# Adaptive-norm columns in fewer, wider tiles, with the projection pieces spread over the next tile and TensorE's order fixed

## The chip, the cores and the metric

One Trainium2 chip, one core. The metric is the device time of one execution in microseconds (us). The kernel before took 1053.7 us (median of 3 runs, 1052.96 to 1055.31).

## The reference

One decoder layer on 256 tokens of width 2048: an adaptive norm, a fused input projection, four attention mixers, an output projection, and a mixture of 16 experts. What the change touches is the beginning:

```python
c_act = jax.nn.silu(c)
mod = c_act @ ada_w[l] + ada_b[l]                    # (1, 2048) @ (2048, 12288)
sh1, sc1, g1, sh2, sc2, g2 = jnp.split(mod, 6, axis=-1)
h = rmsnorm(x, norm1_g[l]) * (1.0 + sc1[:, None]) + sh1[:, None]
proj = h @ w_in_l                                    # the first step of token_mixer
```

All is float32. sc1 and sh1 are matrix-vector products with 2048 x 2048 weights each; h must be complete in a 128-wide block of the width before that block can enter the projection.

## The kernel before

**The early stage.** The width of 2048 is 16 blocks k of 128. The loop over j = 0 to 7 makes two blocks of sc1 and two of sh1 at a time: `ada_tile` (L288) cuts the 2048 x 256 weights of such a tile into 4 units of 512 KB, each with 4 contraction blocks of 256 columns (rows of 1 KB in memory). `ada_acc` (L484) multiplies a unit: for each contraction block k one fp32 matmul with c as the 32-wide stationary operand, placed at column position 32 * (k % 4) of the array, so that the four blocks of a unit stand on four positions. All 16 blocks of a tile add up in one PSUM bank, "ada", which has one buffer. ScalarE copies the sum out (L501), `ada_cols` (L515) adds the four partial sums in small matmuls, and VectorE turns them into columns (L522), adds the bias (L523) and, for sc1, the gain (L526). In the loop `ada_cols` also takes its bank from "ada" (ATAG).

**The hidden state.** `norm1` makes the token norms, `x_transposes` turns x into blocks xT, and `hidden` applies scale and shift and splits each block into a high part Hh and a low part Hl.

**Early pieces.** While the columns are made, TensorE already multiplies finished blocks with parts of the input projection: `early_unit` k is 1024 columns of w_in for one block (rows of 4 KB), and the tiles 4 and SIXTH of w_in come in pieces of 4 blocks by 256 columns (rows of 1 KB). Each piece is split into high and low (`halves`: ScalarE L584, VectorE L586) into two buffers, and `three` (L558) issues three full-width matmuls for each product: 24 matmuls a piece, 23 pieces in all. `bias_tiles` i (16 of them, 16 matmuls each, bank "S") build the attention bias and have no part in the columns. Of the two buffers of "S" one is held by an early accumulator.

**Loads.** All weights come in one list of units, in the order of use, on the SyncE queue into a ring of 11 slots of 512 KB. A slot is free when its unit has been multiplied (columns) or split (pieces); the next load of the list then goes out.

**Order.** The program is written in the order of the loops. A scheduler places the instructions of each engine at build time with a simulated timeline; instructions that are ready in it go first, earlier ones of the program ahead of later ones. `behind` adds an edge of order between two instructions without a wait. `Batch` uses it to keep the matmuls of a unit together. Nothing ties one unit to the next, or to the pieces. The stage ends with the loop's last pieces (blocks 14 and 15, and the last piece of tile 4); then come the gate columns of mixer D (L704) and the rest of the projection.

Of the kernel before, what the change touches and what calls it, by code (L numbers as in the profile page):

```python
# [21 lines left out]
S = 256  # L22
# [158 lines left out]
def hybrid_trunk_kernel(  # L181
# [8 lines left out]
    def behind(ins, other):  # L190

        tc.add_manual_dep(ins, other.name, mybir.DependencyInfo(
            mybir.DependencyClass.NoSync, mybir.DependencyReason.DATA), reason="order")

    class Batch:

        prev = None

        def __call__(self, op, *args, **kw):
            if self.prev is None:  # L200
                ins = op(*args, **kw).ins  # L201
            else:
                with tc.high_priority():
                    ins = op(*args, **kw).ins  # L204
                behind(ins, self.prev)
            self.prev = ins

# [79 lines left out]

    def ada_tile(key):  # L288
        return ada_units(acol[key[0]] + 256 * key[1], key, 256, 4)

# [8 lines left out]
    units = []  # L299
    for j in range(8):  # L300
        units += ada_tile(("sc1", j))
        if j == 0:
            units += [(None, lambda t=t: nc.sync.dma_start(x0[t], x[0, 128 * t:128 * t + 128, :])) for t in range(2)]
        units += [early_unit(2 * j)] + ada_tile(("sh1", j)) + [early_unit(2 * j + 1)]
        if j % 2:
            units.append(win_units(4)[j // 2])
        elif j:
            units.append(win_units(SIXTH)[j // 2 - 1])

# [248 lines left out]
    def three(o, wh, wl, hh, hl, first, last, wstat):  # L558

        if wstat:  # L560
            ins = mm(o, wl, hh, start=first, stop=False)  # L561
            mm(o, wh, hl, start=False, stop=False)  # L562
            mm(o, wh, hh, start=False, stop=last)  # L563
        else:
            ins = mm(o, hh, wl, start=first, stop=False)  # L565
            mm(o, hl, wh, start=False, stop=False)  # L566
            mm(o, hh, wh, start=False, stop=last)  # L567
        return ins.ins
# [53 lines left out]

    def hidden(j):
        for k in (2 * j, 2 * j + 1):
            hs = attp.tile([128, 256], F32, name="hs", tag="hs", bufs=2)
            V.tensor_scalar(hs, xT[:, k, :], A1[:, k:k + 1], B1[:, k:k + 1], OP.mult, OP.add)
            A.copy(Hh[:, k, :], hs[:])
            V.tensor_tensor(Hl[:, k, :], hs[:], Hh[:, k, :].bitcast(F32), OP.subtract)

    for j in range(8):  # L630
        ev = None
        for u in range(4):
            ev = ada_acc(("sc1", j), [u], ev, 4, 256)
        if j == 0:
            norm1()
        else:
            early_mms(2 * j - 2)
        x_transposes(2 * j)
        bias_tiles(2 * j)
        ada_cols(ev, 2, A1[:, 2 * j:2 * j + 2], 16 + 2 * j, g1n[:, 2 * j:2 * j + 2], tag=ATAG)  # L640
        early_split(2 * j)
        ev = None
        for u in range(4):
            ev = ada_acc(("sh1", j), [u], ev, 4, 256)
        bias_tiles(2 * j + 1)
        ada_cols(ev, 2, B1[:, 2 * j:2 * j + 2], 2 * j, tag=ATAG)
        hidden(j)
        if j:
            early_mms(2 * j - 1)
        if j and j % 2 == 0:  # L650
            early_mms5(4, j // 2 - 1)
        early_split(2 * j + 1)
        if j % 2:
            if j > 1:
                early_mms5(SIXTH, j // 2 - 1)
            early_split5(4, j // 2)
        elif j:
            early_split5(SIXTH, j // 2 - 1)
    for k in (14, 15):
        early_mms(k)  # L660
    early_mms5(4, 3)

# [1010 lines left out]
```

## Time and profile before

| | |
|---|---|
| median of 3 runs | 1053.7 us |
| profiled execution | 1056.39 us, span 1054.6 us |
| TensorE busy | 960.3 us, 91% of the span |
| weight loads of TensorE | 582.9 us |
| VectorE busy | 500.4 us, 47% |
| ScalarE busy | 353.1 us, 33% |
| moved by DMA | 371.14 MB, mean 352 GB/s |

The span goes from the first to the last instruction of one profiled execution; the time of that execution is 1.8 us longer. PE is TensorE's matmuls, DVE VectorE, ACT ScalarE, SP SyncE (SPq its DMA queue). Matmuls are pipelined and their ends modelled, so one row's duration is longer than the distance to the next row. TensorE records an fp32 matmul with a 32-wide or 64-wide stationary operand as two passes, that is two rows.

### The profile page before, as it was taken

Reading aid. Unit: us, or ns where it says so; the run is one execution under the profiler, and the core shown is the slowest. Engines: PE = TensorE matmul, PEld = TensorE weight load, DVE = VectorE, ACT = ScalarE, POOL = GpSimd, SP = SyncE. Lnnn points to the kernel's source line nnn. Section 1 sums busy time; section 2 is a strip of 40 time slices with the busy share of each in tenths; the row PEclk is TensorE's granted clock in tenths of the full one; section 3 lists DMA queues with packets and bytes.
Section 4 is the critical chain, followed back from the end, with each engine's and each line's share of the span. In section 5 each row is a group of like instructions: output and inputs, shape, how many; then the busy total and the mean of one; then the engine's idle time right before and its main releaser. Section 6 shows DMA issues by size and latency. Waiting matters only on the chain.

```text
span 1054.6 us, 16417 instructions
## 1 busy us (share of the span) xinstructions
PE 960.3 (91%) x6465; PEld 582.9 (55%) x6465; DVE 500.4 (47%) x1006; ACT 353.1 (33%) x763; POOL 4.8 (0%) x14
## 2 busy tenths in 40 slices
PE   5899999999999998989998999999889897899994
PEld 1677778898788985656784433433243232433323
DVE  2444566996998998344445231414024040422215
ACT  3333344566776768534444101100010000200013
POOL 0000000000000000000000000000000000000000
PEclk9999999999999999999998999999999999999998
DMA  9999999996999999889653999999999999999994
GB/s 332 357 358 359 357 323 325 355 373 210 335 325 348 325 384 387 307 270 384 228 214 145 341 421 414 412 417 415 422 407 421 412 420 413 419 419 414 421 359 128
DMA packets 153596, 371.14 MB, mean 352 GB/s; under 512 B 11514, under 2 KB 90275, under 8 KB 136875
## 3 DMA queue, kind: packets, MB, share of 16 engines
q1 hardware_dynamic: 152512, 368.41, 94.2%
q10 hardware_dynamic: 938, 1.61, 0.4%
q8 instruction: 53, 0.87, 0.3%
q14 instruction: 29, 0.23, 0.1%
q0 software_dynamic: 64, 0.02, 0.0%
HBM read 367.91 MB, written 2.10 MB: 351 GB/s over the span
## 4 chain that ended last, share of the span: by engine, by line
PE 66%; DMA 15%; DVE 8%; ACT 5%; issue 4%; SPq 0%; DVEq 0%; ACTq 0%
PE dn L201 10%; DMA ugu<-in_exp_w_up_dram 9%; PE acc L561 5%; PE acc L562 4%; PE acc L563 4%; PE gatep L201 4%; PE upp L201 3%; PE ada L201 3%; PE upp L204 3%; DMA r<-in_exp_w_up_dram 3%; PE oacc L565 3%; PE pg L1410 3%; PE oacc L566 3%; PE oacc L567 3%; PE gatep L204 2%
## 5 line engine op out<-in xcount | busy, mean ns | idle before, releaser
L561 PE MATMUL acc<-Hh,wlo 128*128 128x256 f32 x512 | 145.7, 294 | 6.3 <-DVE wlo L586 3.9
L562 PE MATMUL acc<-Hl,whi 128*128 128x256 f32 x512 | 146.1, 288 | 0.0
L563 PE MATMUL acc<-Hh,whi 128*128 128x256 f32 x512 | 145.2, 286 | 0.0
L586 DVE TENSOR_TENSOR wlo<-r,whi 128x1024 fp32r<-128x1024 f32 x85 | 103.8, 1221 | 62.7 <-ACT whi L584 60.1
L584 ACT CAST whi<-r 128x1024 fp32r<-128x1024 f32 x85 | 88.9, 1047 | 77.2 <-PE acc L563 28.7
L561 PEld LDWEIGHTS acc<-Hh,wlo 128*128 128x128 f32 x512 | 96.3, 192 | 16.9 <-DVE wlo L586 7.0
L562 PEld LDWEIGHTS acc<-Hl,whi 128*128 128x128 f32 x512 | 98.6, 193 | 3.5 <-issue 2.6
L563 PEld LDWEIGHTS acc<-Hh,whi 128*128 128x128 f32 x512 | 98.6, 193 | 2.7 <-issue 2.3
L511 DVE SCALAR_TENSOR_TENSOR ada_v<-r,cT,ada_v 128x1024 f32<-128x1024 f32 x75 | 95.9, 1279 | 0.4
L204 PE MATMUL upp<-ugu,xg 128*64 128x512 f32 x220 | 90.7, 597 | 4.4 <-DMA ugu<-in_exp_w_up_dram 4.4
L1464 DVE TENSOR_TENSOR he<-upp,sg 128x128 f32<-128x128 f32 x32 | 7.1, 282 | 180.0 <-PE upp L204 180.0
L204 PE MATMUL gatep<-ugu,xg 128*64 128x512 f32 x192 | 82.2, 601 | 0.5 <-DMA ugu<-in_exp_w_gate_dram 0.5
L1543 ACT CAST yhl<-yo 128x512 fp32r<-128x512 f32 x31 | 19.1, 618 | 164.1 <-DVE yo L1537 136.8
L204 PE MATMUL gatep<-r,xg 128*64 128x512 f32 x176 | 71.1, 596 | 0.9 <-DMA r<-in_exp_w_gate_dram 0.9
L201 PE MATMUL dn<-udh,heT 128*64 128x512 f32 x140 | 68.0, 599 | 1.0 <-DVE heT L1481 1.0
L1494 DVE TENSOR_TENSOR xt<-xt,sco 128x512 f32<-128x512 f32 (+1 forms) x70 | 42.1, 637 | 55.4 <-PE sco L1493 54.9
L204 PE MATMUL upp<-r,xg 128*64 128x512 f32 x148 | 65.7, 596 | 2.6 <-DMA r<-in_exp_w_up_dram 2.6
L204 PE MATMUL dn<-udh,heT 128*64 128x512 f32 x140 | 67.6, 599 | 0.0
L1460 ACT ACTIVATE sg<-gatep 128x512 f32<-128x512 f32 x8 | 4.8, 597 | 167.9 <-PE gatep L204 167.9
L565 PE MATMUL oacc<-wlo,Oh 128*128 128x512 f32 (+1 forms) x160 | 58.8, 369 | 0.2
L201 PE MATMUL dn<-r,heT 128*64 128x512 f32 (+1 forms) x124 | 55.5, 558 | 1.6 <-DVE heT L1481 1.6
L567 PE MATMUL oacc<-whi,Oh 128*128 128x512 f32 (+1 forms) x160 | 56.8, 355 | 0.0
(404 smaller groups left out, 1909.0 us busy)
## 6 DMA issues: line engine op xcount, KB each, us to landing
r<-in_ada_w_dram SPq DMA_DIRECT2D x156, 512.0 KB, 7.6
udh<-in_exp_w_down_dram SPq DMA_DIRECT2D x70, 512.0 KB, 11.4
r<-in_w_in_dram SPq DMA_DIRECT2D x69, 512.0 KB, 7.3
ugu<-in_exp_w_up_dram SPq DMA_DIRECT2D x34, 1024.0 KB, 14.6
ugu<-in_exp_w_gate_dram SPq DMA_DIRECT2D x33, 1024.0 KB, 13.8
r<-in_exp_w_gate_dram SPq DMA_DIRECT2D x31, 1024.0 KB, 13.0
r<-in_exp_w_up_dram SPq DMA_DIRECT2D x30, 1024.0 KB, 14.3
r<-in_exp_w_down_dram SPq DMA_DIRECT2D x56, 512.0 KB, 11.4
```

Source lines behind the costliest of these rows:

```text
L201: ins = op(*args, **kw).ins
L204: ins = op(*args, **kw).ins
L511: V.scalar_tensor_tensor(acc, w, cT[:, u:u + 1], acc[:], OP.mult, OP.add)
L561: ins = mm(o, wl, hh, start=first, stop=False)
L562: mm(o, wh, hl, start=False, stop=False)
L563: mm(o, wh, hh, start=False, stop=last)
L565: ins = mm(o, hh, wl, start=first, stop=False)
L566: mm(o, hl, wh, start=False, stop=False)
L567: mm(o, hh, wh, start=False, stop=last)
L584: A.copy(hi, w)
L586: V.tensor_tensor(lo, w, hi[:].bitcast(F32), OP.subtract)
L1494: V.tensor_tensor(y(t, cs), y(t, cs), o, OP.add)
```

## The change

The first norm columns come in five tiles, two of 256 columns and three of 512 (TILES). A unit stays at 512 KB: of a wide tile it has 2 contraction blocks of 512 columns, rows of 2 KB, and there are 8 units each for sc1 and sh1. The pieces of a tile's blocks are no longer issued beside the next units of the same loop, but spread among the units of the next tile by `tile_plan`: a piece is loaded and split ahead of a unit and multiplied behind it. The pieces of the last tile (five) follow at the end. `ada_cols` takes its bank from "S". `chained` ties TensorE's units and pieces into one order, that of the loads: the first matmul of each goes behind the last of the one ahead. Transposes follow units n and n + 2 of a tile (n units each for sc1 and sh1), bias tiles the odd units, up to 4, 6, 9, 12 and 16 by the end of each tile.

```diff
--- before.py
+++ after.py
@@ -192,6 +192,15 @@
         tc.add_manual_dep(ins, other.name, mybir.DependencyInfo(
             mybir.DependencyClass.NoSync, mybir.DependencyReason.DATA), reason="order")
 
+    chain = [None, False]
+
+    def chained(ins, first=False):
+
+        if chain[1]:
+            if first and chain[0] is not None:
+                behind(ins, chain[0])
+            chain[0] = ins
+
     class Batch:
 
         prev = None
@@ -199,10 +208,12 @@
         def __call__(self, op, *args, **kw):
             if self.prev is None:
                 ins = op(*args, **kw).ins
+                chained(ins, True)
             else:
                 with tc.high_priority():
                     ins = op(*args, **kw).ins
                 behind(ins, self.prev)
+                chained(ins)
             self.prev = ins
 
 
@@ -285,8 +296,38 @@
 
     acol = {"sh1": 0, "sc1": 2048, "g1": 4096, "sh2": 6144, "sc2": 8192, "g2": 10240}
 
-    def ada_tile(key):
-        return ada_units(acol[key[0]] + 256 * key[1], key, 256, 4)
+
+    TILES = ((0, 2), (2, 2), (4, 4), (8, 4), (12, 4))
+
+    def ada_tile(nm, t):
+        k0, n = TILES[t]
+        return ada_units(acol[nm] + 128 * k0, (nm, t), 128 * n, 8 // n)
+
+    def tile_pieces(t):
+
+        if t < 0:
+            return []
+        k0, n = TILES[t]
+        ps_ = [("e", k) for k in range(k0, k0 + n)]
+        if (k0 + n) % 4 == 0:
+            ps_.insert(1, ("w", 4, k0 // 4))
+            if k0 < 12:
+                ps_.insert(3, ("w", SIXTH, k0 // 4))
+        return ps_
+
+    def piece_unit(p):
+        return early_unit(p[1]) if p[0] == "e" else win_units(p[1])[p[2]]
+
+    def tile_plan(t):
+
+        n = 2 * TILES[t][1]
+        adas = [(nm, u) for nm in ("sc1", "sh1") for u in range(n)]
+        pcs = tile_pieces(t - 1)
+        plan = []
+        for i, a in enumerate(adas):
+            plan += [p for q, p in enumerate(pcs) if (q + 1) * 2 * n // (len(pcs) + 1) == i]
+            plan.append(("a", i) + a)
+        return plan
 
     def ada_block(key):
         nm, b, width = key
@@ -297,15 +338,12 @@
                                               [(nm, 2 * h, 512), (nm, 2 * h + 1, 512)])]
 
     units = []
-    for j in range(8):
-        units += ada_tile(("sc1", j))
-        if j == 0:
-            units += [(None, lambda t=t: nc.sync.dma_start(x0[t], x[0, 128 * t:128 * t + 128, :])) for t in range(2)]
-        units += [early_unit(2 * j)] + ada_tile(("sh1", j)) + [early_unit(2 * j + 1)]
-        if j % 2:
-            units.append(win_units(4)[j // 2])
-        elif j:
-            units.append(win_units(SIXTH)[j // 2 - 1])
+    for t in range(len(TILES)):
+        for it in tile_plan(t):
+            units.append(ada_tile(it[2], t)[it[3]] if it[0] == "a" else piece_unit(it))
+            if t == 0 and it[2:] == ("sc1", 3):
+                units += [(None, lambda t=t: nc.sync.dma_start(x0[t], x[0, 128 * t:128 * t + 128, :])) for t in range(2)]
+    units += [piece_unit(p) for p in tile_pieces(len(TILES) - 1)]
 
     nw = len(wtiles)
     wkeys = [u[0] for i in range(NEARLY, nw) for u in win_units(i)[3 * (i == SIXTH):]]
@@ -560,11 +598,13 @@
         if wstat:
             ins = mm(o, wl, hh, start=first, stop=False)
             mm(o, wh, hl, start=False, stop=False)
-            mm(o, wh, hh, start=False, stop=last)
+            end = mm(o, wh, hh, start=False, stop=last)
         else:
             ins = mm(o, hh, wl, start=first, stop=False)
             mm(o, hl, wh, start=False, stop=False)
-            mm(o, hh, wh, start=False, stop=last)
+            end = mm(o, hh, wh, start=False, stop=last)
+        chained(ins.ins, True)
+        chained(end.ins)
         return ins.ins
 
     zero = attp.tile([128, 512], BF, name="zero")
@@ -620,45 +660,63 @@
                 P.transpose(pt[:, i, 128 * t:128 * t + 128], x0[t][:, 128 * (k + i):128 * (k + i) + 128], ident)
         V.tensor_tensor(xT[:, k:k + 2, :], pt[:], rxb[:].unsqueeze(1).broadcast_to([128, 2, 256]), OP.mult)
 
-    def hidden(j):
-        for k in (2 * j, 2 * j + 1):
+    def hidden(k):
+        if True:
             hs = attp.tile([128, 256], F32, name="hs", tag="hs", bufs=2)
             V.tensor_scalar(hs, xT[:, k, :], A1[:, k:k + 1], B1[:, k:k + 1], OP.mult, OP.add)
             A.copy(Hh[:, k, :], hs[:])
             V.tensor_tensor(Hl[:, k, :], hs[:], Hh[:, k, :].bitcast(F32), OP.subtract)
 
-    for j in range(8):
-        ev = None
-        for u in range(4):
-            ev = ada_acc(("sc1", j), [u], ev, 4, 256)
-        if j == 0:
-            norm1()
-        else:
-            early_mms(2 * j - 2)
-        x_transposes(2 * j)
-        bias_tiles(2 * j)
-        ada_cols(ev, 2, A1[:, 2 * j:2 * j + 2], 16 + 2 * j, g1n[:, 2 * j:2 * j + 2], tag=ATAG)
-        early_split(2 * j)
-        ev = None
-        for u in range(4):
-            ev = ada_acc(("sh1", j), [u], ev, 4, 256)
-        bias_tiles(2 * j + 1)
-        ada_cols(ev, 2, B1[:, 2 * j:2 * j + 2], 2 * j, tag=ATAG)
-        hidden(j)
-        if j:
-            early_mms(2 * j - 1)
-        if j and j % 2 == 0:
-            early_mms5(4, j // 2 - 1)
-        early_split(2 * j + 1)
-        if j % 2:
-            if j > 1:
-                early_mms5(SIXTH, j // 2 - 1)
-            early_split5(4, j // 2)
-        elif j:
-            early_split5(SIXTH, j // 2 - 1)
-    for k in (14, 15):
-        early_mms(k)
-    early_mms5(4, 3)
+    def split_piece(p):
+        early_split(p[1]) if p[0] == "e" else early_split5(p[1], p[2])
+
+    def piece_products(p):
+        early_mms(p[1]) if p[0] == "e" else early_mms5(p[1], p[2])
+
+    def scale_cols(t, ev):
+        k0, n = TILES[t]
+        ada_cols(ev, n, A1[:, k0:k0 + n], 16 + k0, g1n[:, k0:k0 + n], tag="S")
+
+    def shift_cols(t, ev):
+        k0, n = TILES[t]
+        ada_cols(ev, n, B1[:, k0:k0 + n], k0, tag="S")
+        for k in range(k0, k0 + n):
+            hidden(k)
+
+    chain[1] = True
+    bias_at, made = (4, 6, 9, 12, 16), 0
+    for t, (k0, nblk) in enumerate(TILES):
+        ev, pend, n = None, None, 2 * nblk
+        for it in tile_plan(t):
+            if it[0] != "a":
+                split_piece(it)
+                pend = it
+                continue
+            i, nm, u = it[1:]
+            if u == 0:
+                ev = None
+            ev = ada_acc((nm, t), [u], ev, 8 // nblk, 128 * nblk)
+            if pend:
+                piece_products(pend)
+                pend = None
+            if t == 0 and i == n - 1:
+                norm1()
+            if i == n - 1:
+                scale_cols(t, ev)
+            if i == 2 * n - 1:
+                shift_cols(t, ev)
+            if i in (n, n + 2) and i - n < nblk:
+                x_transposes(k0 + i - n)
+            if i % 2 and made < bias_at[t]:
+                bias_tiles(made)
+                made += 1
+    rest = tile_pieces(len(TILES) - 1)
+    split_piece(rest[0])
+    for q, p in enumerate(rest):
+        if q + 1 < len(rest):
+            split_piece(rest[q + 1])
+        piece_products(p)
+    chain[1] = False
 
 
     qkv = {}
```

## Rows read from the trace of the kernel before

**Rows 1.** The page, busy tenths of 40 slices of the span:
```profile
PE   5899999999999998989998999999889897899994
...
DMA  9999999996999999889653999999999999999994
```

**Rows 2.** Stretches: length, busy PE, PEld, DVE, ACT, POOL, clock, DMA share, GB/s:
```profile
0.00:50.00 50.00, 33.50 (x329) 18.51 (x330) 18.40 (x57) 19.23 (x41) 1.73 (x8) 0.97 1.02 344
30.00:130.00 100.00, 93.51 (x1116) 70.62 (x1108) 44.53 (x102) 34.80 (x69) 0.00 (x0) 0.98 1.09 358
385.00:410.00 25.00, 24.64 (x194) 19.40 (x194) 24.71 (x45) 19.06 (x47) 0.00 (x0) 1.00 1.05 386
40.00:60.00 20.00, 17.76 (x216) 12.91 (x206) 8.41 (x19) 6.67 (x14) 0.00 (x0) 0.91 1.09 357
```

**Rows 3.** Who TensorE waited for, 20 to 160 us: total, times, longest:
```profile
PE ada L201 <- DMA r<-in_ada_w_dram: 6.6, 3, 5.9
PE ada L201 <- DVE ada_ev L522: 2.5, 4, 0.9
...
PE ada_c L520 <- ACT ada_ev L501: 2.0, 3, 0.9
...
PE S L553 <- DVE xT L621: 1.3, 1, 1.3
PE xtr L620 <- DVE TD L556: 1.2, 2, 0.7
```

**Rows 4.** Timeline of TensorE: start, duration, line, operation, idle before:
```profile
20.38 0.61 PE L201 MATMUL ada<-r,cB 128*32 128x256 f32 x1 [5.85 <-DMA r<-in_ada_w_dram]
...
44.20 0.61 PE L201 MATMUL ada<-usc,cB 128*32 128x256 f32 x1 [1.29 <-DVE B L523]
```

**Rows 5.** Who the SyncE queue waited for, 20 to 160 us:
```profile
SPq L219 <- PE ada L204: 31.8, 28, 4.5
```

**Rows 6.** Timeline of TensorE, end of the early stage:
```profile
145.06 0.39 PE L204 MATMUL ada<-r,cB 128*32 128x256 f32 x3
145.99 0.32 PE L520 MATMUL ada_c<-ada_ev,kc 128*32 128x64 f32 x8 [0.54 <-ACT ada_ev L501]
148.38 0.74 PE L561 MATMUL acc<-Hh,wlo 128*128 128x256 f32 x4 [2.07 <-ACT Hh L627]
...
157.21 1.92 PE L704 MATMUL gacc<-Hh,uw 128*24 128x256 f32 x30
```

**Rows 7.** Who TensorE waited for, 157 to 240 us:
```profile
PE acc L561 <- DVE wlo L586: 1.4, 1, 1.4
```

**Rows 8.** Timeline of TensorE, a column unit between products:
```profile
60.05 0.28 PE L563 MATMUL acc<-Hh,whi 128*128 128x256 f32 x1
...
60.26 0.42 PE L204 MATMUL ada<-r,cB 128*32 128x256 f32 x3
...
60.50 0.39 PE L204 MATMUL ada<-r,cB 128*32 128x256 f32 x3
...
60.83 0.38 PE L561 MATMUL acc<-Hh,wlo 128*128 128x256 f32 x1
```

**Rows 9.** Timeline of TensorE, a bias tile between two column units:
```profile
83.03 0.54 PE L553 MATMUL S<-tabs,line 105*128 105x32 bf16 x15
83.50 0.40 PE L201 MATMUL ada<-r,cB 128*32 128x256 f32 x1
```

**Rows 10.** Timeline of TensorE, two passes of two 512-column matmuls, experts:
```profile
568.06 0.59 PE L201 MATMUL gatep<-ugu,xg 128*64 128x512 f32 x1
...
568.49 0.59 PE L201 MATMUL gatep<-ugu,xg 128*64 128x512 f32 x1
```

**Rows 11.** Timeline of TensorE, two neighbouring 512-column units of g1:
```profile
405.79 0.62 PE L201 MATMUL ada<-ug,cB 128*32 128x512 f32 x1
...
405.81 0.62 PE L204 MATMUL ada<-r,cB 128*32 128x512 f32 x2
406.25 0.59 PE L201 MATMUL ada<-ug,cB 128*32 128x512 f32 x1
```

## The prediction

> **What bounds the kernel now.** I read the page's slices first, then stretches of the early stage, then who waits for whom there, then the instructions themselves. In the slices [rows 1], of 26.4 us each, the DMA engines are at 9 tenths in the first nine and TensorE from the third on, and the change lies in the first six. So one must ask which of the two ends last.
>
> The loads run at 358 GB/s from 30 to 130 us with the DMA share over 1 [rows 2]: saturated. TensorE is busy 93.5 of those 100 us [rows 2], and its waits between 20 and 160 us are short and mostly on VectorE and ScalarE; the waits for a load come to 6.6 us [rows 3], 5.9 of them one wait that ends at 20.4 us [rows 4]. The SyncE queue, in turn, waits 31.8 us in 28 pieces for TensorE to give back a column slot [rows 5]. So after about 26 us no landing holds TensorE up, while TensorE's pace holds issues up: TensorE is the bound by a little, with the loads close behind. The end shows it too: the last column unit ends near 145.3 us, the three remaining pieces run from 148.4 to 157.2 us, and the next stage follows without a gap [rows 6]; from 157 to 240 us TensorE waits 1.4 us in all [rows 7]. A microsecond more or less at 157 us is therefore carried on, through a TensorE stage into the experts, whose loads start as buffers come free.
>
> **Prices.** A column unit of 256 columns is four fp32 matmuls, one on each 32-column position of the array. The four start together, and a second pass of all four follows 0.24 us later [rows 8]; in a run of such units each takes 0.43 us. Where a unit stands between products of full width, the way in costs 0.09 us and out 0.12 us (60.05 + 0.12 to 60.26, and 60.50 + 0.21 to 60.83) [rows 8]: 0.21 us a run. Products of a piece are 24 at 0.12 us, 2.9 us a piece: three pieces fill 148.38 to 157.2 us [rows 6]. A bias tile between two units takes 0.47 us for 15 of its 16 matmuls (83.03 to 83.50) [rows 9], 0.57 us with the turn.
>
> **The change, part by part.**
>
> *Wider units.* A 512-column unit of the same bytes holds two contraction blocks, so only two of the four positions. Two 512-column matmuls side by side take 0.43 us a pass, two passes each (the experts' rows at 568.06 and 568.49) [rows 10]: 0.86 us a unit, double. Only if the next unit, with the other two positions, follows directly do the four run together: two such units of different loads at 405.79 us start within 0.02 us and take two passes of about 0.45 us for both [rows 11]. So 48 units cost 48 x 0.43 = 20.6 us now and 20.6 to 41.3 us after.
>
> How many can pair? The new plan puts products behind units 3, 6, 9, 12 of the third tile and behind 2, 4, 6, 9, 11, 13 of the last two, and between units 7 and 8 the accumulator is copied out. Taking neighbours greedily, the third tile needs 10 turns of 0.86 us (6 pairs, 4 alone), each of the last two 9 (7 pairs, 2 alone): 28 turns, 24.1 us. But the loop also places bias tiles behind units 1, 3, 5 (and 7), and transposes behind 8 and 10, and these split pairs: in strict program order 11 + 13 + 13 = 37 turns, 31.8 us. In the trace some such fillers stand between two column units [rows 9] and others elsewhere, so I take the middle, 33 turns: 28.4 us, **+7.7 us** (bounds +3.5 and +11.2).
>
> *Loads.* 48 of the 87 units go from rows of 1 KB to rows of 2 KB. The stretch 385 to 410 us, in which 512-column blocks with rows of 2 KB dominate, ran at 386 GB/s against 358 GB/s [rows 2]. Subtracting the 4 KB rows of the sixteen wide pieces, I estimate 350 GB/s for 1 KB rows: 48 x 0.524 MB at 350 and at 386 GB/s is 71.9 and 65.2 us, 6.7 us sooner. TensorE is the bound, so this goes into loads that lie ready in the eleven slots, and I cost it at **nothing**; the cover is TensorE's backlog, and if that were gone the 6.7 us would count.
>
> The Trainium skill ("DMA: Bandwidth & Descriptors", "Specifications") gives 512 B as the minimum transfer for line rate. By it 1 KB rows would have lost nothing, and the load term would be zero in every case; the two rates in [rows 2] disagree.
>
> *Spread pieces and their order.* The same 23 pieces of 2.9 us are multiplied; five instead of three are left behind the last column unit (14.5 against 8.8 us). As TensorE is the bound, that is work moved, not added. On the SyncE queue the same 87 loads are issued, five instead of two behind the last column unit. At the start: up to the second tile's last column unit the new queue has 18 units and x, some 12 MB with the constants; at 344 GB/s (0 to 50 us) [rows 2] they land by 35 to 38 us. TensorE then has 16 column units and two pieces behind it, as at 41 us now: **0**. Six bias tiles instead of three are done by then, in time that waits for loads anyway: 3 x 0.57 = **-1.7 us**.
>
> *Column turns.* Ten turns instead of sixteen, each with a copy out and a small matmul group. The waits at turns now are 2.5 + 2.0 us [rows 3] and the last turn's, the rest covered by pieces. After, no piece may fill in, as the chain fixes the order; behind a waiting column unit all of TensorE's chained work queues. The last turn waited 0.54 us for a 256-column copy [rows 6]; with 512 columns I estimate 0.8 us, so six wide and two narrow turns wait 5.9 us against some 5: **0**, within 2 us either way.
>
> *Other waits.* The 1.2 us for the bias bank [rows 3] should fall away with one bank of its own for the columns: **-1.2 us**, at most -2.5 with the 1.3 us on xT. The granted clock was 0.91 from 40 to 60 us [rows 2]; TensorE had waited 1.29 us before 44.20 us [rows 4], and at the lower of its two levels, 1.2 for 2.4 GHz, 0.09 x 20 = 1.8 us are lost. The same thin stretch exists after, so I take half: **-0.9 us**. The longer chain at the end (copy and group of 512 columns): **+0.3 us**.
>
> Sum: 7.7 - 1.7 - 1.2 - 0.9 + 0.3 = **+4.2 us** at the end of the early stage, passed on. The profiled execution took 1056.39 us (span 1054.6, 1.8 around it): 1060.6 us against it. It stood 2.7 us over the median, so the prediction is 1053.7 + 4.2 = 1057.9 us.
>
> **Rivals.**
>
> *Faster: the pairs hold and the order pays.* At 28 turns, with the fillers placed in the copy-out waits (-2), all of -2.5 and -1.8: 3.5 - 1.7 - 2.5 - 1.8 - 2.0 + 0.3 = -4.2 us, 1049.5 us. If TensorE then keeps up with the loads, up to the 6.7 us can show: 1047 us. For it: 6.5 us of idle between 30 and 130 us [rows 2] that a better order could use. Against it: fillers in program order. It decides below about 29 turns.
>
> *No change.* The early stage moves by a few us, and the stage behind it gives that back: loads lie further ahead, so VectorE can take its weight and column work in the longer tail. Against it: TensorE is at 9 tenths or more there [rows 1] with 1.4 us of waits [rows 7]. 1053.7 us, within 2.
>
> *Neighbours don't overlap.* If the second unit's first pass can only follow the first unit's first pass, two adjacent units take three passes, 1.29 us, not two. The 15 pairs among 48 units in 33 turns then cost 15 x 0.43 = 6.5 us more: +10.7, 1064.4 us. The start times in [rows 11] speak against it. The Trainium skill ("TensorE: Matmul & The Clock Gate", Part 3, "The mechanism") says that matmuls start and end strictly in program order, without reordering; emitted unit by unit this is what that would do, and the trace agrees only if the four were laid out pass by pass.
>
> *The clock stays low.* TensorE would wait for loads between 23 and 41 us, and after a wait the unit at 44.20 us took 0.61 us a pass where others take 0.40 [rows 4, 8]; two pieces at the lower level are 5.8 us more of work, of which I let some 3.6 reach the end: 1061.5 us. I count it into the upper part of the range.
>
> **How the numbers follow.** Part of the pairs (the forecast) 0.37, with its own range 1055 to 1061.5; neighbours that don't overlap, or no pairs at all, 0.13; no change 0.20; faster 0.30. A difference under 0.2% (2.1 us) cannot be told from none. The forecast and the non-overlap case are slower: 0.50; same 0.20; faster 0.30. The range runs from 1048.5 (the favourable case with some of the loads' gain) to 1064.5 us (non-overlap).
>
> **What would show it.** In the profile after: 512-column units with passes 0.43 us apart, alone (0.86 us) or four matmuls together; some 33 turns; loads near 370 GB/s and the slot wait of the SyncE queue larger, not smaller; no long load waits of TensorE after 41 us; last column unit near 142 us, first matmul of the next stage near 161 us instead of 157.2. Wrong, if TensorE waits for landings throughout (then the loads were the bound), if the next stage starts before 156 us, or if that shift is not found again at the first expert matmul.

## The result, and the profile after

The changed kernel took 1084.65 us (median of 4 runs, 1082.34 to 1088.05) against 1054.51 us for the kernel before: a ratio of 1.0272 (95% interval 1.0240 to 1.0304), 30 us slower. The forecast was 1057.9 us in a range of 1048.5 to 1064.5 us: the direction was right, the size far too small. The profiled execution has a span of 1081.0 us, 26.4 us more than before: 11.3 us are lost by the first matmul of the gate columns, 10.9 from there to the output projection, 2.5 to the experts and 1.7 behind them.

The page of the changed kernel, TensorE and DMA in the slices [rows 1]:

```profile
PE   5798989699899999897998999899879898898994
...
DMA  9998998689799999988853899999999999999993
```

(Slices of 27.0 us.) Stretches as in [rows 2], with the same columns, and one of the stage that follows:

```profile
0.00:50.00 50.00, 32.57 (x320) 17.81 (x324) 16.28 (x52) 18.82 (x41) 1.74 (x8) 0.93 1.01 343
30.00:130.00 100.00, 89.14 (x826) 62.48 (x825) 41.96 (x87) 30.76 (x57) 0.00 (x0) 0.93 0.98 341
40.00:60.00 20.00, 17.73 (x208) 13.04 (x209) 7.72 (x19) 7.05 (x14) 0.00 (x0) 0.90 1.01 361
190.00:230.00 40.00, 30.74 (x270) 27.18 (x269) 26.59 (x56) 18.05 (x33) 0.53 (x1) 0.87 0.69 236
```

Who TensorE waited for, 26.3 to 168 us [rows 3], and below it the SyncE queue, 20 to 160 us [rows 5]:

```profile
PE acc L599 <- ACT Hh L667: 3.8, 4, 1.9
PE acc L600 <- DVE Hl L668: 2.3, 3, 1.0
PE ada_c L558 <- ACT TD L594: 1.7, 1, 1.7
PE ada_c L558 <- DVE xT L661: 1.7, 2, 0.9
PE S L591 <- DVE ada_ev L560: 1.6, 4, 0.5
PE ada L210 <- ACT ada_ev L539: 1.5, 3, 0.7
PE ada_c L558 <- ACT ada_ev L539: 1.5, 2, 0.7
PE S L591 <- DVE xT L661: 0.5, 1, 0.5
```

```profile
SPq L230 <- PE ada L214: 44.6, 21, 7.1
SPq L295 <- PE ada L214: 18.1, 7, 3.6
```

No row names a landing, as none did in the kernel before after 26.3 us. The 14.6 us (10.4 in the kernel before, from 26.3 us to its gate columns) are what surrounds a column turn: the copies, the columns, then the hidden halves Hh and Hl, then the first products. The waits for TD and xT (3.9 us) are for bank "S": the bias tiles and the transposes of x, which the columns now share it with, had to be copied out of it first. And the SyncE queue waits longer for TensorE's column units (44.6 + 18.1 us in the two rows shown, against 31.8 us in [rows 5] and 3.7 us in a row not shown there), so the loads run slower from 30 to 130 us, 341 against 358 GB/s. The timeline of TensorE, at the first turns and at the end of the stage [rows 6]:

```profile
13.05 0.61 PE L591 MATMUL S<-tabs,line 105*128 105x32 bf16 x16
...
24.09 1.19 PE L518 MATMUL S<-dg,ones 128*128 128x128 f32 x4 [1.37 <-DVE dg L517]
...
26.07 0.44 PE L558 MATMUL ada_c<-ada_ev,kc 128*32 128x64 f32 x8
...
33.72 0.44 PE L558 MATMUL ada_c<-ada_ev,kc 128*32 128x64 f32 x8 [1.68 <-ACT TD L594]
...
35.80 0.58 PE L599 MATMUL acc<-Hh,wlo 128*128 128x256 f32 x1 [0.69 <-ACT Hh L667]
37.16 0.58 PE L600 MATMUL acc<-Hl,whi 128*128 128x256 f32 x1 [0.78 <-DVE Hl L668]
37.54 0.41 PE L601 MATMUL acc<-Hh,whi 128*128 128x256 f32 x1
37.76 0.41 PE L599 MATMUL acc<-Hh,wlo 128*128 128x256 f32 x1
...
147.64 0.59 PE L210 MATMUL ada<-r,cB 128*32 128x512 f32 x1
147.64 0.59 PE L214 MATMUL ada<-r,cB 128*32 128x512 f32 x1
147.65 0.59 PE L210 MATMUL ada<-r,cB 128*32 128x512 f32 x1
147.66 0.59 PE L214 MATMUL ada<-r,cB 128*32 128x512 f32 x1
...
152.06 0.38 PE L599 MATMUL acc<-Hh,wlo 128*128 128x256 f32 x1 [1.92 <-ACT Hh L667]
...
168.46 0.85 PE L762 MATMUL gacc<-Hh,uw 128*24 128x256 f32 x12
```

The first scale columns wait behind a bias tile and the token norms, which have bank "S" ahead of them: they come at 26.07 us. In the kernel before the same matmuls stood in bank "ada" at 14.08 us:

```profile
14.08 0.44 PE L520 MATMUL ada_c<-ada_ev,kc 128*32 128x64 f32 x8 [0.49 <-ACT ada_ev L501]
```

The shift columns at 33.72 us wait 1.68 us for that bank again. From there to 37.16 us one turn costs TensorE the three waits shown and 0.37 us ahead of a bias tile, and the products after them come 0.21 us apart instead of 0.12 us until 40.3 us: the lower of the two clock levels (granted 0.50). Stretches of the changed kernel at that level:

```profile
33.80:40.50 6.70, 4.86 (x40) 4.32 (x41) 3.44 (x9) 2.32 (x5) 0.00 (x0) 0.50 1.08 373
54.30:57.60 3.30, 3.18 (x14) 3.01 (x15) 1.15 (x4) 1.06 (x4) 0.00 (x0) 0.50 1.03 402
85.00:88.30 3.30, 3.30 (x17) 3.28 (x16) 2.11 (x4) 1.49 (x3) 0.00 (x0) 0.50 1.08 374
153.20:156.50 3.30, 3.30 (x18) 3.30 (x17) 2.95 (x5) 0.68 (x2) 0.00 (x0) 0.50 1.12 340
```

Each begins in or behind the waits of a shift turn. Together they are 17 us; the kernel before has one such stretch, of 3.4 us (44.2 to 47.6 us). The four rows at 147.64 us are two neighbouring 512-column units that overlap on all four positions, as [rows 11] had it. The stage ends at 168.46 us, 11.3 us later than before.

Then as much again is lost. TensorE and, below it, the SyncE queue from 200 us on:

```profile
213.87 1.09 PE L941 MATMUL pcTp<-ident,pc 128*128 128x128 f32 x4 [6.65 <-DVE vc L901]
216.23 0.58 PE L599 MATMUL acc<-Hh,wlo 128*128 128x256 f32 x1 [1.27 <-DVE wlo L626]
```

```profile
200.86 0.38 SPq L248 DMA_DIRECT2D uw<-in_w_in_dram  x1
211.54 0.38 SPq L248 DMA_DIRECT2D r<-in_w_in_dram  x1
```

That is mixer D's compression, whose small steps TensorE, VectorE and ScalarE pass to each other. From the vcp matmuls (206.8 us) to these transposes TensorE has no piece; in the kernel before three stood there (191.0 to 202.7 us). No load goes out for 10.7 us, TensorE stands for 6.65 us, and the stretch from 190 to 230 us moves 236 GB/s. From the gate columns to the output projection TensorE's waits of over 0.15 us come to 18.2 us, against 8.1 us before: 10.1 of the 10.9 us.

### The profile page after: what moved, and what is told of

It reads as the page before. It is cut to its first block, busy times and chain, and to the rows that moved or that the text cites. A ratio compares the mean times of both kernels' runs of the same rounds, so it can differ in the third digit from the quotient of the medians.

```text
span 1081.0 us, 15910 instructions
## 1 busy us (share of the span) xinstructions
PE 968.8 (90%) x6225; PEld 584.3 (54%) x6225; DVE 501.5 (46%) x991; ACT 355.6 (33%) x759; POOL 4.8 (0%) x14
## 4 chain that ended last, share of the span: by engine, by line
PE 68%; DMA 15%; DVE 8%; ACT 5%; issue 3%; SPq 0%; ACTq 0%; DVEq 0%
PE dn L210 10%; DMA ugu<-in_exp_w_up_dram 7%; PE acc L599 5%; PE acc L600 4%; PE acc L601 4%; PE gatep L210 4%; PE ada L210 4%; PE upp L210 4%; PE upp L214 3%; DMA r<-in_exp_w_up_dram 3%; PE oacc L603 3%; PE pg L1468 3%; PE oacc L604 3%; PE oacc L605 3%; PE gatep L214 3%
## 5 line engine op out<-in xcount | busy, mean ns | idle before, releaser
L599 PE MATMUL acc<-Hh,wlo 128*128 128x256 f32 x512 | 154.9, 303 | 8.3 <-DVE wlo L626 4.4
L600 PE MATMUL acc<-Hl,whi 128*128 128x256 f32 x512 | 149.3, 292 | 2.4 <-DVE Hl L668 2.3
L601 PE MATMUL acc<-Hh,whi 128*128 128x256 f32 x512 | 148.8, 291 | 0.0
L626 DVE TENSOR_TENSOR wlo<-r,whi 128x1024 fp32r<-128x1024 f32 x81 | 98.9, 1222 | 59.1 <-ACT whi L624 59.0
L599 PEld LDWEIGHTS acc<-Hh,wlo 128*128 128x128 f32 x512 | 101.5, 198 | 26.6 <-issue 10.7
L624 ACT CAST whi<-r 128x1024 fp32r<-128x1024 f32 x81 | 84.5, 1048 | 85.3 <-PE acc L601 24.3
L600 PEld LDWEIGHTS acc<-Hl,whi 128*128 128x128 f32 x512 | 101.6, 198 | 3.6 <-DVE Hl L668 3.5
L601 PEld LDWEIGHTS acc<-Hh,whi 128*128 128x128 f32 x512 | 101.4, 198 | 1.6 <-issue 1.6
L210 PE MATMUL dn<-udh,heT 128*64 128x512 f32 x140 | 69.5, 612 | 0.5 <-DVE heT L1539 0.5
L214 PE MATMUL dn<-udh,heT 128*64 128x512 f32 x140 | 69.1, 612 | 0.0
L210 PE MATMUL ada<-r,cB 128*32 128x512 f32 (+1 forms) x140 | 53.2, 587 | 9.9 <-DMA r<-in_ada_w_dram 8.2
L214 PE MATMUL ada<-r,cB 128*32 128x512 f32 (+1 forms) x244 | 59.8, 583 | 0.0
## 6 DMA issues: line engine op xcount, KB each, us to landing
ugu<-in_exp_w_up_dram SPq DMA_DIRECT2D x34, 1024.0 KB, 14.7
ugu<-in_exp_w_gate_dram SPq DMA_DIRECT2D x33, 1024.0 KB, 13.7
```

What stands on the lines that cost most here:

```text
L601: end = mm(o, wh, hh, start=False, stop=last)
L624: A.copy(hi, w)
L626: V.tensor_tensor(lo, w, hi[:].bitcast(F32), OP.subtract)
```

## The experiments

Three landmarks are the starts of TensorE's first matmul of the gate columns (end of the early stage), of the output projection and of the experts. The medians stand beside those of the kernel before on the same chip.

```
                      us      before   ratio (95%)             gate   output  experts
before                1054.5                                   157.2  401.8   561.2
after                 1084.7  1054.5   1.0272 (1.0240-1.0304)  168.5  424.0   585.9
e1_no_chain           1074.6  1056.2   1.0157 (1.0117-1.0197)  168.2  417.9   577.6
e2_chain_before       1051.8  1056.2   0.9948 (0.9922-0.9974)  151.0  399.2   556.7
e3_narrow_tiles       1086.9  1056.2   1.0278 (1.0238-1.0318)  180.0  432.0   590.4
e4_transposes_later   1079.7  1056.2   1.0190 (1.0147-1.0233)  169.0  427.0   585.6
e5_products_at_turns  1060.9  1056.9   1.0031 (1.0012-1.0050)  159.5  407.3   565.2
e6_at_turns_narrow    1077.8  1056.9   1.0168 (1.0130-1.0207)  174.7  425.1   585.1
e7_extra_matmuls      1087.5  1056.9   1.0268 (1.0232-1.0304)  182.4  437.9   596.8
e8_one_piece_later    1069.3  1056.5   1.0122 (1.0082-1.0163)  165.8  413.2   572.9
e9_stream_first       1085.3  1056.5   1.0269 (1.0230-1.0308)  168.7  423.8   586.2
e10_turns_other_bank  1063.1  1056.5   1.0059 (1.0028-1.0091)  160.5  407.4   566.0
e11_steps_on_time     1075.5  1054.3   1.0208 (1.0176-1.0239)  169.2  414.7   579.6
e12_half_loads_after  1087.6  1054.3   1.0309 (1.0279-1.0339)  179.2  433.3   592.5
e13_half_loads_before 1052.6  1054.3   0.9966 (0.9944-0.9988)  141.1  397.4   557.5
```

TensorE's time from 26.3 us to the gate columns by what it works on, from the first run of rows that starts behind 26.3 us, each run counted up to the start of the next (a few matmul records are missing). A wait ahead of a run is therefore part of the run before it. The last two columns are TensorE's waits of over 0.15 us, those ahead of piece products and all:

```
            units  columns  bias tiles  transposes  pieces  (ahead of pieces, all waits)
before      32.2   12.0      8.7        4.4         73.2    2.1  10.4
after       36.9    6.6     11.5        6.2         80.4    6.2  14.6
e1          45.3    7.0     10.5        5.6         73.3    5.8  12.7
e2          33.8    8.3      8.2        5.4         68.8    0.0   7.5
e3          43.7    7.1     12.8        6.0         83.8    6.9  24.9
e5          38.7    3.7     10.6        4.7         74.8    2.0   9.2
e6          28.8    7.2     17.6        6.1         88.5   12.4  21.9
e8          42.4    6.6      9.9        4.9         75.5    3.0   9.2
e10         46.8    4.4      7.4        5.4         70.3    0.0   8.8
e12         38.0    9.7     13.8       12.0         79.3    6.7  25.6
e13         25.4    4.3      7.3        3.0         74.6    1.5   1.9
```

**Which part of the change.** Without the fixed order:

```diff
-    chain[1] = True
+    chain[1] = False
```

> The changed kernel with the fixed TensorE order switched off, wide tiles and spread pieces kept. Theory A (fixed order leaves the column turns without cover, TensorE idles there and its clock falls): the early stage, which ends at 168.5 us in the changed kernel and at 157.2 us before, ends at 157 to 161 us, and the piece products in it take about 73 us instead of 80. Theory B (the wide units fill half the array, and that is the loss): it still ends at 164 us or later. The mixer-D transposes stand behind three pieces again in this kernel, so the middle stage should lose nothing: total 1054 to 1058 us under A, 1061 to 1066 under B.

The early end stayed (168.2 us): the pieces fell back to 73.3 us, but the units rose to 45.3 us. Ten us came back behind the stage, so the total, too, fits neither theory. The fixed order alone, put into the kernel before (with `chained` as in the change):

```diff
+    chain[1] = True
     for j in range(8):
...
     early_mms5(4, 3)
+    chain[1] = False
```

> The kernel before with the fixed order alone: narrow tiles, pieces where the old loop has them. Theory A (it is the lack of pieces at the turns, not the fixing as such): the old loop has a piece behind most turns, so the early stage ends within 4 us of 157.2 and the total is 1052 to 1059 us. Rival (fixing the order costs by itself, since no stall can be filled): it ends at 163 us or later, total 1060 or more.

With all its loads in place it is the one version faster than both kernels, by 0.5%. So the fixed order by itself isn't the loss. The changed kernel with eight narrow tiles (the numbers of bias tiles by the end of each tile, `bias_at`, follow them: 4, 6, 8, 9, 11, 12, 14, 16):

```diff
-    TILES = ((0, 2), (2, 2), (4, 4), (8, 4), (12, 4))
+    TILES = tuple((k, 2) for k in range(0, 16, 2))
...
```

> The changed kernel with eight tiles of 256 columns instead of two and three: spread pieces and fixed order kept, no unit fills half the array. Theory A: 16 turns without cover instead of 10, so the early stage ends no earlier than 166 us although the units take some 5 us less. Theory B: the 4.7 us that the units cost go away and more, it ends at 158 to 163 us. In both the middle stage should lose nothing, as the mixer-D transposes stand behind pieces: A 1063 us or more, B 1056 to 1061.

No faster, with an early end even 11.5 us later: the width isn't the main loss either. What is left is where the pieces stand, and the bank of the turns.

**Where the pieces stand.** The products go to the column turns, all else kept:

```diff
-            if pend:
-                piece_products(pend)
-                pend = None
...
-            if i == n - 1:
-                scale_cols(t, ev)
-            if i == 2 * n - 1:
-                shift_cols(t, ev)
+            if i % n == n - 1:
+                if pend:
+                    piece_products(pend.pop(0))
+                (shift_cols if i >= n else scale_cols)(t, ev)
+                while pend:
+                    piece_products(pend.pop(0))
...
```

> The changed kernel with one thing moved: the products of each early piece are issued at the column turns (the first piece ahead of the scale or shift columns, the rest right behind them) and no longer among the units. Tiles, loads, splits, fixed order are those of the changed kernel. If the placement is the cause (turns without work behind them, a lower clock after them, the pieces that follow paying), the granted clock of 26 to 168 us goes back above 0.97, the piece products of the early stage cost about 73 us and not 80, the first gate column comes at about 156 us and not 168, and the total is within 10 us of the kernel before. If the wide units themselves are the cause, the first gate column stays near 165 us and the total above 1072. If the late order of the loads is the cause, the early stage gains at the turns, but the 11 us of the stage with mixer D's compression (157 to 220 us) stay: a total of about 1070.

It brings back 24 of the 30 us: the early end at 159.5 us, columns 3.7, pieces 74.8 and all waits 9.2 us. Nine of the 24 us are back at the gate columns; 7.7 are the next stage's, where three pieces stand between the vcp matmuls and the transposes again. The granted clock did not come back (0.93 from 26 to 150 us), so that part of the expectation failed. The same with the narrow TILES of the run above:

> As the run with the products at the turns, but with eight tiles of 256 columns in place of two of 256 and three of 512. With good placement this gives the price of the width alone. By the sum of the prediction the wide units cost 7.7 us and six turns fewer give back little, so this one would be 5 to 8 us faster than its wide twin; by the narrow-tile run among the units (no faster than wide) it would be the same or up to 5 us slower, as it has six more turns of scale and shift columns.

17 us slower than its wide twin: neither of the two prices expected. The units cost 9.9 us less than in the wide twin, but the pieces 13.7 and the bias tiles 7.0 us more, most of it waits (21.9 against 9.2 us): here sixteen turns cost more than wide units do in ten. Why the turns wait so much longer wasn't tested. The turns' bank back to "ada" in e5 (for the scale columns, too):

```diff
-        ada_cols(ev, n, B1[:, k0:k0 + n], k0, tag="S")
+        ada_cols(ev, n, B1[:, k0:k0 + n], k0, tag=ATAG)
...
```

> The kernel with the products at the turns (1060.9 us), with its column turns back in the bank that the kernel before uses for them (that of the units) and not in the one that the bias tiles, the transposes of x and the columns share. TensorE waited 4.8 us for the copies of the bias tiles there. If the shared bank is what is left of the loss, these waits go and the total falls by 3 to 5 us, to that of the kernel before or below; if the units then wait for the columns' transposes instead, or the loads set the end of the early stage, it stays within 2 us of 1060.9.

No gain in total: the bank alone isn't what is left. But it moved the start: the scale columns of the first tile came at 14.6 us as in the kernel before (14.9 us) and not at 27.0 us, and blocks 0 to 3 had their shift columns at 44.4 instead of 52.7 us. By block 11 that was lost again (110.4 against 105.1 us): the runs of units, with the waits behind them, took 8.1 us more. Products one piece later in the changed kernel, still among the units:

```diff
-            if pend:
-                piece_products(pend)
-                pend = None
+            if len(late) > 1:
+                piece_products(late.pop(0))
...
```

> The changed kernel with the products of every early piece issued one piece later in TensorE's order: a piece is split when its load comes in the plan, and its products follow only when the next piece has been split. The places among the units, the loads, the tiles and the turns stay. If the changed kernel loses because a piece's products follow its split (and the hidden halves) too closely, the 6.2 us in which TensorE waits ahead of piece products fall to about 2, less is lost at the loads that wait for slots, the first gate column comes at about 162 us and the total at about 1075. If the loss is the place in the middle of the units itself (turns without work behind them), the early end stays at 167 to 170 us and the total at 1080 to 1087.

The waits ahead of pieces fell from 6.2 to 3.0 us, yet the early end moved by only 2.7 us, as the units took 5.5 us more. The total fell by 15 us, most of it behind the stage, where the scheduler now placed the compression steps otherwise; so this run doesn't separate the two.

**The clock.** Matmuls that add zeros, 4 ahead of each scale turn, 8 ahead of each shift turn:

```diff
+    def keep_busy(times):
+        for _ in range(times):
+            ins = mm(early[0][:].rearrange("p c n -> p (c n)"), zero[:, 0:128], zero[:], start=False, stop=False)
+            chained(ins.ins, True)
...
```

> The changed kernel with extra work for TensorE: 4 matmuls of 512 zero columns ahead of each scale turn and 8 ahead of each shift turn, added as zeros to a bank in use, 60 in all (about 13 us of work at the full clock, if none of it falls into a wait). If the lower clock is what the turns cost, the granted clock of 26 to 168 us rises from 0.94 to above 0.97, the piece products fall from 80 back toward 73 us, and the first gate column comes no more than 6 us later in spite of 13 us of added work. If the clock isn't it, the early stage grows by all the 13 us and the pieces stay at 80.

The early end came 14 us later for 12.1 us of such matmuls, the pieces stayed at 80.5 us and the clock at 0.93 (26 to 182 us; 0.94 from 26 to 168 us in the changed kernel). So filling the turns this way isn't a cure: TensorE's waits did not shrink (15.7 against 14.6 us), those ahead of pieces were 8.4 instead of 6.2 us. It doesn't show what the lower clock by itself costs.

**The stage behind.** Mixer D's transposes behind the newest piece:

```diff
+                behind(tr.ins, lastpiece[0])
```

> The changed kernel with one edge of order more: the mixer-D transposes (pcTp) go behind the first matmul of the newest piece, so that pieces stand between the values' small matmuls (vcp) and them. Theory C (10.9 us of the loss are this one place in the order, where TensorE waits 6.6 us with pieces queued behind it): the early stage ends at 168.5 us as in the changed kernel, the first output-projection matmul comes at 413 to 416 us instead of 424, total 1073 to 1077 us. Rival (the loss there comes from late loads, whatever the order): first output-projection matmul at 421 us or later, total 1081 or more.

The expected gain in this stage didn't come (424.0 to 427.0 us at the output projection): the stall moved to a piece that waited 9.0 us for its split. Two ties for VectorE and ScalarE (exponential behind the last cast, its product behind the last vector unit):

```diff
+                behind(ins, recent["hi"])
...
+                behind(ins, recent["v"])
```

> The changed kernel with two order ties in the stage of mixer D's compression, and nothing else: on VectorE the second half of the softmax chain goes behind the vector unit of the late norm columns that the trace shows waiting behind it (at 210.23 us), and on ScalarE the exponential goes behind the last cast of a piece. If the stage loses because VectorE and ScalarE hold the load stream's slots behind that chain (SP without a free slot from 200.9 to 211.5 us, 14 GB/s from 205 to 210 us), the transfers go on, the early end stays at 168 us, and the first output-projection matmul comes some 8 us earlier than 424 us: a total of about 1075. If the stage loses because too little had been loaded by its beginning, whatever the order, the wait only moves and the total stays at 1081 to 1087.

Moved again: TensorE now waited 5.4 us for a split, up to 212.0 us. Then TensorE's order of the whole compression, each step ahead of the piece after the next:

```diff
+            newest = recent[-1] if recent else None
             piece_mms(pn)
+            ahead[0] = newest
...
+                if cc == 0 and kk == 0 and ahead[0] is not None:
+                    behind(ins, ahead[0])
```

> The changed kernel with mixer D's compression steps tied on TensorE: the matmuls of a step (the z, part, hid, kcp and vcp matmuls) go ahead of the products of the piece after the next, so that none is left three or four pieces late. The order from 168 us on is then that of the kernel before (vcp, two or three pieces, the transposes), the early stage is untouched. If the order of that stage is what costs its 11 us, the early end stays at 168 us, the first output-projection matmul comes at about 413 us and not 424, and the total at about 1073. If it is the state of the loads at the early end, the stage still loses its 11 us and the total stays at 1080 to 1087.

The early end stayed, the stage took 245.5 us to the output projection (169.2 to 414.7) as in the kernel before (244.6) and not 255.5 us, and 9 us came back. Two pieces stand between the vcp matmuls and the transposes here. Its stretch, beside that of after from 190 to 230 us shown above:

```profile
190.00:230.00 40.00, 37.65 (x338) 34.38 (x337) 34.98 (x72) 22.22 (x45) 0.53 (x1) 0.96 0.94 317
```

**Loads or TensorE.** Half of the early columns' bytes, in both kernels (`got` is half of a unit's contraction blocks; the matmuls use them twice):

```diff
-                t.rearrange("p (k n) -> p k n", k=kn), adaT[:, kn * u:kn * u + kn, col:col + n])
+                t.rearrange("p (k n) -> p k n", k=kn)[:, 0:got], adaT[:, kn * u:kn * u + got, col:col + n])
...
```

> The changed kernel with half of the early norm columns' bytes left out: every unit loads half of its rows and its matmuls use them twice, so the scale and shift columns are not the reference's; all matmuls, copies and turns stay. It takes 16.8 MB of the some 55 MB away that are loaded by the early end. If the early end is a sum on TensorE, as the prediction took it, the first gate column stays at 165 to 168 us. If transfers that wait for slots set it, it falls to about 150 us (the early stage's TensorE time without its waits is some 127 us after 26 us).

> The kernel before with the same half of the early norm columns' bytes left out (its scale and shift columns are not the reference's). If transfers set both kernels' early ends, this one also falls from 157 to about 145 us or earlier, and the gap between the two kernels shrinks from 11 us to what TensorE's own order costs (about 5 us by units, bias tiles and turns). If TensorE sets both, it stays at 155 to 157 us and the gap stays at 11 us.

The times at which VectorE adds the bias to the shift columns of the blocks up to 3, 7, 11 and 15 (the starts of the rows that write B), and the gate columns, with four of the runs above:

```
            3      7      11      15      gate
before     43.9   80.3   113.7   146.7   157.2
e13        37.3   66.9    98.3   129.3   141.1
after      53.3   81.3   117.3   151.0   168.5
e12        53.1   85.4   121.7   162.1   179.2
e5         52.7   77.2   105.1   139.8   159.5
e10        44.4   74.8   110.4   140.9   160.5
e1         54.6   78.6   111.9   150.3   168.2
e2         45.2   76.2   106.6   140.2   151.0
```

Neither theory had this pair. The kernel before fell by 16 us, 13 of them within the first 80 and 5 by its first shift columns (29.2 to 24.1 us); its waits went from 10.4 to 1.9 us. Transfers that held its start would do this. But the scheduler, too, chose another order for every engine, and order alone, with all the bytes, moved the same end by 6.2 us (e2), so the share of each isn't shown. Its first gate matmul, and what TensorE waited for most up to 141 us and from there to 240 us:

```profile
141.10 0.42 PE L705 MATMUL gacc<-Hh,uw 128*24 128x256 f32 x4
```

```profile
PE acc L562 <- DVE wlo L587: 1.5, 1, 1.5
...
PE acc L562 <- DVE wlo L587: 8.2, 1, 8.2
```

The changed kernel did not fall at any of these points; it ended at 179.2 us, with longer waits of the kind it had (20 to 179 us):

```profile
PE ada_c L559 <- DVE xT L662: 6.6, 2, 5.8
PE acc L600 <- ACT Hh L668: 5.8, 4, 2.8
PE S L592 <- DVE ada_ev L561: 3.7, 4, 2.5
PE ada_c L559 <- ACT TD L595: 3.5, 1, 3.5
```

All its waits are 25.6 us, 11.0 more than in the changed kernel, and all are for ScalarE and VectorE. So fewer bytes didn't bring its early end forward. That bytes have no part in it is not shown: with other loads the scheduler also orders VectorE and ScalarE anew, and of TensorE's work only units and pieces are fixed. Why the hand-overs came so much later stays open.

## Why the prediction was wrong, step by step

**"After about 26 us no landing holds TensorE up": in doubt for the start.** With half the bytes the kernel before is 16 us earlier at the gate columns, 11 of them behind 29 us. The rows of waits couldn't show this, as none names a DMA after 26.3 us; the time stands in runs of units (32.2 against 25.4 us) and turns (12.0 against 4.3 us). How much of it is bytes and how much order is open (above). The SyncE queue's 31.8 us of waits for TensorE were read as showing who is behind, but somebody frees every slot, and the changed kernel, slower, has more of them.

**"At the start ... 0": wrong.** Blocks 0 to 3 had their columns 9.4 us later (53.3 against 43.9 us), and with half the bytes no sooner. It is the bank: without the fixed order they came at 54.6 us (e1), with the fixed order alone at 45.2 (e2), and with the turns back in "ada" at 44.4 instead of 52.7 us (e10 against e5). The first wide tile regained it (81.3 against 80.3 us).

**"... one bank of its own for the columns: -1.2 us": wrong.** "S" is no bank of its own: the bias tiles, the token norms and the transposes of x use it. The waits for TD and xT grew from 2.5 to 3.9 us, and the first scale columns came 12 us late. In exchange the units lost their waits for the columns in "ada" (2.5 + 1.3 us), of which 1.6 us came back as waits of bias tiles in "S".

**"Column turns: 0, within 2 us": the step that failed.** The prediction saw that "no piece may fill in" and that "behind a waiting column unit all of TensorE's chained work queues", and then priced a turn by the copy alone. What stands at a shift turn is longer: the transposes of x in the same bank, small matmuls, Hh, Hl, and only then products. All waits grew by 4.2 us. The pieces grew by 7.2 us, 2.3 of it waits between their rows; the other 4.9 us fit the lower clock behind the turns, where 14.7 us of the pieces stood instead of 1.6 us. (An estimate: 13.1 us of products 0.21 instead of 0.12 us apart are 5.6 us.) The columns fell by 5.4 us. Moving only the products, to the turns, returned 9 of the 11.3 us (e5), 5.4 of them waits.

**"Work moved, not added": wrong with it.** From the last shift columns to the gate columns it is 17.5 us instead of 10.5 us, five pieces for three, and the columns weren't earlier for it but 4.3 us later. The pieces cost the same matmuls but no longer cover the turns, and the bias tiles, priced at -1.7 us, cost +2.8 us, all of it the waits that end their runs, for the bank among others.

**Wider units, +7.7 us: right in kind, smaller.** Units cost +4.7 us, 1.4 of it waits. Of the 48 wide units 36 stand in pairs and 12 alone, at 0.86 us each: 30 turns where 33 were forecast. The rival without overlap is out: the four passes at 147.64 us start within 0.02 us. The rule of the Trainium skill ("TensorE: Matmul & The Clock Gate", Part 3, "The mechanism") that matmuls start and end strictly in program order would give three passes if the units are issued one after the other; the trace agrees with it only if the four are laid out pass by pass.

**Loads at nothing: not contradicted in the changed kernel,** though for another reason than given: its slots came free late and its loads ran slower (341 against 358 GB/s), so the 2 KB rows had nothing to gain, and half the bytes brought nothing (e12).

**The clock, -0.9 us and a rival at +3.6 us:** the rival had the sign, and its 5.8 us of added work are near the 4.9 us of the pieces. But the lower level did not come from waits for loads: its 17 us begin in or behind the waits of shift turns. Filling the turns with zeros didn't remove it.

**"A microsecond more or less at 157 us is carried on": half wrong, and by size as large a miss as the turns.** A later end was carried on and then doubled: 10.9 us more in the compression stage, priced at nothing, whose order the scheduler had changed (tying it returned 9, e11). An earlier end is partly given back: 16.1 us at the gate columns in e13 were 4.4 at the output projection and 1.7 in the medians, since the next stage then waited 8.2 us for a split; 6.2 us in e2 were 2.6 there and 4.4 in the medians.

Open: the last 4 us of e5, and why narrow tiles at the turns (e6) lose so much more with the late loads. The price of the wide units alone, with the loads of the kernel before, wasn't measured.

## What to carry to other kernels

Before products are moved from one place of a fixed order to another, ask what they covered where they stood: the chain from the last unit of a tile to its first usable product, through each engine, is the price of an uncovered turn. Before a buffer is given to other work, ask who holds it when that work is ready. Where loads and the engine run close together, idle rows may not tell which one is the bound; halving the bytes in one run tells more, if the order of every engine is held. And an edit to one stage can reorder the next where a scheduler places the instructions: compare the order of the instructions behind the edit, too.

## What the runs showed that was not expected

A fixed order of TensorE by itself made the kernel before 0.5% faster (e2). Filling matmuls at the turns did not raise the granted clock of the stage (0.93 with 60 of them, 0.94 without). One tag, the bank of the column turns, decided when the first blocks were ready (44.4 against 52.7 us), and yet the total did not gain (e10).
